# The end of a decoder step: written ahead of the branch for left-over blocks and once more behind it, with one tile summed on TensorE

## The chip, the cores and the metric

The kernel runs on one core of a Trainium2 chip. The metric is device microseconds of one execution, the median of several runs. A profiled execution of the same program gives the trace that is read here; its times count from the start of its span.

## The reference, cut to what matters

The whole step is one decoder layer: a prompt of 512 rows and 8 sample rows of 1024 columns go through attention, a convolution group and a mixture of experts. Only its last lines are touched by the change:

```python
def rmsnorm(x, g):
    x32 = x.astype(jnp.float32)
    y = x32 * lax.rsqrt(jnp.mean(x32 * x32, axis=-1, keepdims=True) + EPS)
    return (y * g.astype(jnp.float32)).astype(x.dtype)
...
    x = x + mods[2] * mix
    h = rmsnorm(x, norm2_g) * (1.0 + mods[4]) + mods[3]
    return x + mods[5] * hier_moe(h, ...)      # top 2 of 8 experts in the best of 4 groups
...
    y_prompt = rmsnorm(xp, final_g)
    y_sample = rmsnorm(xs, final_g)
```

Every row gets the products of two experts. The sum of the residual row and its two expert rows is scaled by the inverse root of its mean square and by `final_g`.

## The kernel before, in words

Everything is in one core's program; a framework orders the instructions of each engine by its own model of time and puts in the semaphores. Where the order of one engine matters the code pins it with `tc.issue_after`.

**The expert loop.** Rows are grouped by expert into blocks of 64. There are 32 experts and four static second blocks, 36 blocks in all (`OV0`), and up to 16 more (`MAXX`) for rows that did not fit. `run` (L1611) goes through the 36: `weights` (L1530) reads 3 MB for each expert on SyncE's queue into pages, a rotating pool of 21 buffers (`page`, L195); `turned` and `up` make the two hidden products on TensorE, `hidden` (L1575) a Silu on ScalarE and a product on VectorE, `flip` and `down` the last product. `down` scatters the block's result from `ot` into the DRAM tensor `yrow`, with an indirect DMA on Pool's queue (L1600). `yrow` has four rows of 512 columns for every token: two experts times two halves. The residual is in the DRAM tensor `xrow`.

**The left-over blocks.** After the loop `gf` (`final_g`) and the four residual tiles `xt` are asked for on SyncE. All engines read a count (`nxi`, L1798) and branch on it (L1799). If it is over 0 the 16 left-over blocks run with weights gathered by indirect DMAs. With the inputs given it is 0 and the blocks are skipped. What a skipped block would have counted up on the semaphores is made up for at the end of the branch, at the same line.

**The end.** Behind the branch come L1805 to L1863. The 512 prompt rows are four tiles of 128 rows and 1024 columns. SyncE reads, for each, two halves of `yt` (L1813, one for each expert, 512 KB), and after tile 1's the eight sample rows in four small DMAs (`ysq`, L1816). `total(i)` (L1820) adds the two halves to the residual on VectorE (L1822, L1826), ScalarE squares and sums the result (L1827), VectorE adds EPS (L1832 or L1830) and Pool takes the power -1/2 (L1833). `final(i)` (L1836) scales on VectorE (L1845) and SyncE writes the tile out (L1846). Tile 3 goes in two halves of 512 columns. `sample` (L1848) adds the sample rows on Pool in three operations of 256 columns; `quarter_rstd` (L537) squares them on ScalarE (L540), adds partitions with a small product (L542) and ends in `rsq` (L333), with a power on Pool (L336). VectorE scales them (L1860) and ScalarE's queue writes them in four small DMAs (L1863). The order is "t0 t1 f0 t2 f1 s t3 q f2 f3"; only VectorE's sums, and the finals, the sample and its root against the sum before them, are pinned. L1883 is the closing of the program: drains of all engines and a handshake.

In the middle of the kernel, `tile_start(2)` (L1367) asks for output weights and `mrow`'s rows, and Pool clears the half page `B2b` (L1386, `mB` in the trace), which the expert loop later uses for gathered rows.

Of the kernel before, what the change touches and what calls it, by code (L numbers as in the profile page):

```python
# [9 lines left out]
F32 = mybir.dt.float32  # L10
# [4 lines left out]
ALU = mybir.AluOpType  # L15
# [14 lines left out]
GF_ = ()  # L30
ORD, ISS = "t0 t1 f0 t2 f1 s t3 q f2 f3", "fsq"
GT, TH, TF = (), (1, 1, 1, 2), (1, 1, 1, 2)
# [148 lines left out]
def body(tc, I, O, dbg=lambda *a: None):  # L181
# [13 lines left out]
    def page(name, w=2048):  # L195
        t = pg.tile([128, PW], F32, tag="E", name=name)
        return t[:, :w]
# [1169 lines left out]
    def tile_start(i):  # L1367
# [15 lines left out]
        if i == WOI:  # L1383
            load_wo(0, 2)
            SP.dma_start(A2b, mrow[2:3, :].to_broadcast([128, 1024]))
            G.memset(B2b, 0.0)  # L1386
            for q in range(4):
                SP.dma_start(b2q[32 * q:32 * q + 8].rearrange("p (c j) -> p c j", c=8),
                             mrow[1:2, :].rearrange("o (c r j) -> o c r j", r=4, j=32)[:, :, q].to_broadcast([8, 8, 32]))
            ready.add("A")  # L1390
# [184 lines left out]
    def hidden(b):  # L1575
        pgu = pgus.pop(b)
        hd = hds[b] = small("hd")
        S.activation(hd[64:128], pgu[0:64], AF.Silu)  # L1578
        return V.tensor_tensor(hd[64:128], pgu[64:128], hd[64:128], op=ALU.mult)  # L1579
# [54 lines left out]
    pgus, hds, hTs_, scat = {}, {}, {}, []  # L1634
# [153 lines left out]
    run(todo, asked)  # L1788
    gfq = cp.tile([128, 256], F32, name="gfq", tag="c1")
    with tc.issue_after(mark["S"].ins):  # L1790
        S.dma_start(gfq, I["GFQ"])
# [3 lines left out]
    for i in range(4):  # L1795
        SP.dma_start(half(xt[i // 2], i % 2), xrow[128 * i:128 * i + 128])
    spare = [[page(f"sg{j}"), page(f"su{j}"), page(f"sd{j}")] for j in range(3)]
# [5 lines left out]


    ry = yrow.rearrange("(t a) f -> t (a f)", a=4)  # L1805
    ssf = cp.tile([128, 8], F32, name="ssf")
    rsf = cp.tile([128, 8], F32, name="rsf")
    ysq = mid("ysq").rearrange("p (a f) -> p a f", a=2)
    V.memset(ysq, 0.0)
    yt = [page(f"yt{i}") for i in range(4)]  # L1810
    for i in range(4):
        for j in range(2):
            SP.dma_start(half(yt[i], j), ry[128 * i:128 * i + 128, 1024 * j:1024 * j + 1024])  # L1813
        if i == 1:
            for q in range(4):
                SP.dma_start(ysq[32 * q:32 * q + 8].rearrange("p a (c j) -> p (a c) j", c=8),  # L1816
                             ry[512:520].rearrange("b (x r j) -> b x r j", r=4, j=32)[:, :, q])
    fs = small("fs")

    def total(i):  # L1820
        t, t1, x = half(yt[i], 0), half(yt[i], 1), half(xt[i // 2], i % 2)
        (G if i in GT else V).tensor_tensor(x, x, t, op=ALU.add)  # L1822
        n = 1024 // TH[i]
        for h in range(TH[i]):
            c = slice(n * h, n * h + n)
            op = V.tensor_tensor(t[:, c], x[:, c], t1[:, c], op=ALU.add)  # L1826
            S.activation(t1[:, c], t[:, c], AF.Square, scale=1.0 / 32, accum_out=ssf[:, 2 * i + h:2 * i + h + 1])  # L1827
        r = rsf[:, i:i + 1]
        if TH[i] == 2:
            V.scalar_tensor_tensor(r, ssf[:, 2 * i:2 * i + 1], EPS, ssf[:, 2 * i + 1:2 * i + 2], op0=ALU.add, op1=ALU.add)  # L1830
        else:
            V.tensor_scalar(r, ssf[:, 2 * i:2 * i + 1], EPS, None, op0=ALU.add)  # L1832
        G.tensor_tensor(r, r, mh[:, 0:1], op=ALU.pow)  # L1833
        return op

    def final(i):  # L1836
        n = 1024 // TF[i]
        for h in range(TF[i]):
            c = slice(n * h, n * h + n)
            t = half(yt[i], 0)[:, c]  # L1840
            if i in GF_:
                S.activation(t, t, AF.Copy, scale=rsf[:, i:i + 1])
                G.tensor_tensor(t, t, gfb[:, c], op=ALU.mult)
            else:
                V.scalar_tensor_tensor(t, t, rsf[:, i:i + 1], gfb[:, c], op0=ALU.mult, op1=ALU.mult)  # L1845
            SP.dma_start(O[0][0, 128 * i:128 * i + 128, c], t)  # L1846

    def sample():  # L1848
        G.tensor_tensor(fs, ysq[:, 0], ysq[:, 1], op=ALU.add)  # L1849
        G.tensor_tensor(fs, fs, m5s, op=ALU.mult)  # L1850
        G.tensor_tensor(fs, fs, x1s, op=ALU.add)  # L1851

    op = None
    for nm in ORD.split():
        with tc.issue_after(op.ins) if op is not None and nm[0] in ISS else ExitStack():
            r = (sample() if nm == "s" else quarter_rstd(rsf[:, 4:5], fs, 1.0 / D, EPS) if nm == "q" else
                 total(int(nm[1])) if nm[0] == "t" else final(int(nm[1])))
        if nm[0] == "t":
            op = r
    V.scalar_tensor_tensor(fs, fs, rsf[:, 4:5], gfq, op0=ALU.mult, op1=ALU.mult)  # L1860
    oq = O[1].rearrange("b t (c r j) -> (b t) c r j", r=4, j=32)
    for q in range(4):
        S.dma_start(oq[:, :, q], fs[32 * q:32 * q + 8].rearrange("p (c j) -> p c j", c=8))  # L1863
# [23 lines left out]
```

## Time and profile before

| | us |
|---|---|
| median of 3 runs | 795.29 (792.6 to 795.43) |
| the profiled execution | 790.3 |
| its span | 788.4 |
| PE busy | 688.5 (87%) |
| DVE busy | 452.7 (57%) |
| ACT busy | 205.8 (26%) |
| POOL busy | 203.0 (26%) |

PE is TensorE, DVE VectorE, ACT ScalarE, POOL Pool (GpSimd) and SP SyncE; a name with q is the engine's queue of DMA issues, semaphores and branches. PEclk is the share of TensorE's full clock that was granted. The span is a little shorter than the execution's time, since it runs from the first to the last instruction of the program. The shares of busy time are averages over stages with different limits, so the rows below are from the last 40 us, where the change plays, and a few from other stages for the price of single operations.

### The profile page before, as it was taken

The numbers are of one execution on the slowest core, as the hardware profiler recorded it, in microseconds if no ns is written. First come the engines' busy times: TensorE is split into PE (matmuls) and PEld (weight loads), VectorE is DVE, ScalarE is ACT, GpSimd is POOL, SyncE is SP. The second block draws the span as 40 slices with busy tenths as digits, with TensorE's granted clock in tenths as the row PEclk, the third lists the DMA queues.
The fourth block names the chain that finished last, engine by engine and source line by source line (L and its number), as shares of the span: only waits on it lengthen the run. The fifth ranks groups of instructions, "written<-read, shape, count | busy, mean of one in ns | idle before, by whom it ended". The sixth has DMA issues, their size and how long they took to land. (4 is left out here: it accounts for less than half of the span.)

```text
span 788.4 us, 12678 instructions
## 1 busy us (share of the span) xinstructions
PE 688.5 (87%) x4908; PEld 416.2 (53%) x4908; DVE 452.7 (57%) x995; ACT 205.8 (26%) x475; POOL 203.0 (26%) x183
## 2 busy tenths in 40 slices
PE   5999898998999988999789998389999999999800
PEld 3555887877786445544445445245555555554400
DVE  3445629999984758732777744664444434343335
ACT  1254721111122557543235324020000000000011
POOL 5144205034230101135610202112222222221114
PEclk9999999999998999999979999599999999999965
DMA  9985325645899104500003857789998999999853
GB/s 344 419 347 201 135 81 216 243 160 219 280 382 402 62 2 149 240 0 1 1 16 137 317 194 277 276 307 398 418 380 322 416 418 420 416 419 419 351 195 147
DMA packets 42477, 199.54 MB, mean 253 GB/s; under 512 B 11005, under 2 KB 14477, under 8 KB 22821
## 3 DMA queue, kind: packets, MB, share of 16 engines
q1 hardware_dynamic: 29485, 155.78, 50.8%
q0 software_dynamic: 10336, 40.95, 13.4%
q10 hardware_dynamic: 2592, 1.95, 0.8%
q8 instruction: 41, 0.67, 0.3%
q14 instruction: 23, 0.19, 0.1%
HBM read 187.33 MB, written 22.15 MB: 266 GB/s over the span
## 5 line engine op out<-in xcount | busy, mean ns | idle before, releaser
L591 DVE SCALAR_TENSOR_TENSOR y<-u,c,y 128x511 f32<-128x511 f32 (+23 forms) x120 | 102.0, 882 | 2.1
L1578 ACT ACTIVATE hd<-pgu 64x256 f32<-64x256 f32 x36 | 13.5, 376 | 234.8 <-PE pgu L1573 234.8
L1600 POOL DMA_INDIRECT yrow<-ot,six x36 | 39.2, 1088 | 99.3 <-DVE ot L1599 88.2
L1573 PE MATMUL pgu<-eu,mB 128*64 128x256 f32 x256 | 61.7, 384 | 1.6 <-DMA eu<-in_WU 1.5
L1573 PE MATMUL pgu<-eg,mB 128*64 128x256 f32 x256 | 62.1, 384 | 0.0
L1595 PE MATMUL pd<-ed,hTe 128*64 128x512 f32 x240 | 57.3, 598 | 0.8 <-issue 0.8
L1573 PE MATMUL pgu<-eu,mA 128*64 128x256 f32 x224 | 54.0, 384 | 1.9 <-DMA eu<-in_WU 1.9
L1573 PE MATMUL pgu<-eg,mA 128*64 128x256 f32 x224 | 54.2, 384 | 0.0
L1579 DVE TENSOR_TENSOR hd<-pgu,hd 64x256 f32<-64x256 f32 x36 | 15.4, 428 | 52.4 <-ACT hd L1578 52.3
L1599 DVE SCALAR_TENSOR_TENSOR ot<-pd,wtb,mt 128x512 f32<-128x512 f32 x36 | 27.0, 751 | 31.2 <-PE pd L1595 31.2
L1573 PEld LDWEIGHTS pgu<-eg,mB 128*64 128x64 f32 x256 | 32.9, 136 | 19.7 <-issue 5.9
L225 DVE COPY hTe<-hTp 128x128 f32<-128x128 f32 x36 | 10.5, 291 | 50.2 <-PE hTp L1586 48.9
L1573 PEld LDWEIGHTS pgu<-eg,mA 128*64 128x64 f32 x224 | 28.8, 136 | 17.1 <-issue 5.2
L1423 ACT ACTIVATE P<-pSp,ast 128x128 f32<-128x128 f32 (+3 forms) x64 | 33.2, 535 | 17.3 <-DVE ast L1418 17.0
L370 PE MATMUL pr<-cTs,wc 128*64 128x256 f32 x256 | 36.1, 390 | 0.0
L1418 DVE TENSOR_REDUCE ast<-pSp 128x1 f32<-128x384 f32 (+3 forms) x44 | 27.3, 633 | 14.4 <-PE pSp L1413 14.3
L1573 PEld LDWEIGHTS pgu<-eu,mB 128*64 128x64 f32 x256 | 33.0, 136 | 3.7 <-DMA eu<-in_WU 2.5
L1292 PE MATMUL woA<-wo,qT 128*128 128x512 f32 x64 | 34.3, 652 | 0.2 <-DVE x1a L1295 0.2
L1573 PEld LDWEIGHTS pgu<-eu,mA 128*64 128x64 f32 x224 | 28.9, 136 | 3.5 <-DMA eu<-in_WU 2.5
L1112 PE MATMUL woC<-wo,y 128*128 128x512 f32 x64 | 30.6, 608 | 0.1
L361 PE MATMUL cT<-CI,cR 128*128 128x128 f32 x128 | 20.9, 300 | 10.4 <-DVE cR L386 10.3
L542 PE MATMUL qs<-st,CI 128*128 128x1 f32 x6 | 1.5, 311 | 31.1 <-ACT jks L540 31.1
(582 smaller groups left out, 1694.3 us busy)
## 6 DMA issues: line engine op xcount, KB each, us to landing
eg<-in_WG SPq DMA_DIRECT2D x26, 1024.0 KB
eu<-in_WU SPq DMA_DIRECT2D x26, 1024.0 KB
ed<-in_WD SPq DMA_DIRECT2D x26, 1024.0 KB
wada<-in_WA SPq DMA_DIRECT2D x16, 1024.0 KB
wada<-in_WA POOLq DMA_DIRECT2D x8, 1024.0 KB
WG<-in_WG SPq DMA_DIRECT2D x6, 1024.0 KB
WU<-in_WU SPq DMA_DIRECT2D x6, 1024.0 KB
WD<-in_WD SPq DMA_DIRECT2D x6, 1024.0 KB
```

What stands on the lines that cost most here:

```text
L361: PE.transpose(p[:, j, :], R[b:b + n, c, k, 2 * s8:2 * s8 + 2, :], ident[b:b + n, b:b + n])
L370: mark["PE"] = PE.matmul(self.pr[r][64 * c:64 * c + 64], wc1[:, c, 8 * r + 4 * h + s, :], self.T[h][:, c, s], start=(h == 0 and s == 0), s ...
L591: V.scalar_tensor_tensor(yb[:, s_:CVS], ub[:, :CVS - s_], w(k), yb[:, s_:CVS], op0=ALU.mult, op1=ALU.add)
L1112: PE.matmul(p, zc[:, g, 128 * i:128 * i + 128], wo[2 * n + 1][:, g], start=(g == 0), stop=(g == 3))
L1292: PE.matmul(pA, oTp[:, g, 128 * i:128 * i + 128], wo[2 * n][:, g], start=(g == 0), stop=(g == 3))
L1418: V.tensor_reduce(st[k][:, 0, h0:h0 + nh], pS[k][:, :nh * L].rearrange("p (h l) -> p h l", h=nh), axis=AX.X, op=ALU.max, negate=True)
L1423: S.activation(P[k][:, g, :L], pS[k][:, o:o + L], AF.Exp, bias=st[k][:, 0, g:g + 1], accum_out=st[k][:, 1, g:g + 1])
L1573: chain[0] = PE.matmul(pgus[b][64 * h:64 * h + 64, :], xT[:, c, 64 * s_:64 * s_ + 64], w[:, c, :], start=(c == 0), stop=(c == 7))
L1579: return V.tensor_tensor(hd[64:128], pgu[64:128], hd[64:128], op=ALU.mult)
L1595: chain[0] = PE.matmul(pd[64 * h:64 * h + 64, :], hT_[:, c, :], wd[:, c, 512 * h:512 * h + 512], start=(c == 0), stop=(c == 1))
L1599: V.scalar_tensor_tensor(ot, pd, wtb[:, b:b + 1], mt, op0=ALU.mult, op1=ALU.mult)
L1600: st = G.indirect_dma_start(out=yrow[:, :], out_offset=bass.IndirectOffsetOnAxis(ap=six[:, b:b + 1], axis=0), in_=ot, in_offset=None, boun ...
```

## The change

The end, from the reads of `yt` to the writes, becomes a function `ending`, called twice: right after the 36 blocks, ahead of the count and the branch, and again inside the branch after the left-over blocks, which then writes all outputs anew. So that the first call reads no rows that were never written, SyncE fills `yrow` with zeros from `B2b` in `tile_start(2)`.

Inside `ending`: tile 0 is summed on TensorE as three products with the identity for each half of 512 columns (residual, first expert, second expert) in PSUM; tiles 1 to 3 on VectorE in halves. Each tile of `yt` is read in one DMA of 1 MB. Pool has no work: the sample's three sums are on VectorE, and the power is replaced by `inv_root`, a square root on ScalarE and, on VectorE, a reciprocal with one step of Newton's method. All of VectorE's operations are pinned in the order of the program by `dv`, all of ScalarE's activations by `ac`. One square root of a constant is put behind the loop's last Silu.

```diff
@@ head of the file
-ORD, ISS = "t0 t1 f0 t2 f1 s t3 q f2 f3", "fsq"
+TP = (0,)
@@ tile_start
             G.memset(B2b, 0.0)
+            SP.dma_start(yrow.rearrange("(p a b) f -> p a (b f)", p=104, b=2), B2b[:104].unsqueeze(1).to_broadcast([104, 10, 1024]))
             for q in range(4):
@@ hidden
-        S.activation(hd[64:128], pgu[0:64], AF.Silu)
+        silu[0] = S.activation(hd[64:128], pgu[0:64], AF.Silu)
@@ behind run(todo, asked)
-    with tc.issue_after(mark["S"].ins):
+    with tc.issue_after(silu[0].ins):
         S.dma_start(gfq, I["GFQ"])
...
+    with tc.issue_after(mark["V"].ins):
+        V.memset(ysq, 0.0)
+    with tc.issue_after(silu[0].ins):
+        S.activation(rsf[:, 5:6], one, AF.Sqrt)
+
+    def ending():
+        for i in range(4):
+            SP.dma_start(half(xt[i // 2], i % 2), xrow[128 * i:128 * i + 128])
+        for i in range(4):
+            SP.dma_start(yt[i], ry[128 * i:128 * i + 128])
+            if i == 1:
+                for q in range(4):
+                    SP.dma_start(ysq[32 * q:32 * q + 8].rearrange("p a (c j) -> p (a c) j", c=8),
+                                 ry[512:520].rearrange("b (x r j) -> b x r j", r=4, j=32)[:, :, q])
+        row, arow = [None], [None]
+        def ac(*a, **k):
+            with tc.issue_after(arow[0].ins) if arow[0] is not None else ExitStack():
+                arow[0] = S.activation(*a, **k)
+        def dv(f, *a, **k):
+            with tc.issue_after(row[0].ins) if row[0] is not None else ExitStack():
+                row[0] = f(*a, **k)
+        def inv_root(s_, r, t):
+            ac(t[:, 0:1], s_, AF.Sqrt)
+            dv(V.reciprocal, t[:, 1:2], t[:, 0:1])
+            dv(V.scalar_tensor_tensor, t[:, 0:1], s_, t[:, 1:2], t[:, 1:2], op0=ALU.mult, op1=ALU.mult)
+            dv(V.tensor_scalar, t[:, 0:1], t[:, 0:1], -0.5, 1.5, op0=ALU.mult, op1=ALU.add)
+            dv(V.tensor_tensor, r, t[:, 0:1], t[:, 1:2], op=ALU.mult)
+        py = {i: [acc("py") for _ in range(2)] for i in TP}
+        with in_turn():
+            for i in TP:
+                for h, c in enumerate(cols):
+                    chain[0] = PE.matmul(py[i][h], ident, half(xt[i // 2], i % 2)[:, c], start=True, stop=False)
+        def total(i, hs=(0, 1)):
+            t0, t1, x = half(yt[i], 0), half(yt[i], 1), half(xt[i // 2], i % 2)
+            for h in hs:
+                c = cols[h]
+                if i in TP:
+                    with in_turn():
+                        PE.matmul(py[i][h], ident, t0[:, c], start=False, stop=False)
+                        chain[0] = PE.matmul(py[i][h], ident, t1[:, c], start=False, stop=True)
+                    z = py[i][h]
+                else:
+                    dv(V.tensor_tensor, x[:, c], x[:, c], t0[:, c], op=ALU.add)
+                    dv(V.tensor_tensor, x[:, c], x[:, c], t1[:, c], op=ALU.add)
+                    z = x[:, c]
+                ac(jy[:, c], z, AF.Square, scale=1.0 / 32, accum_out=ssf[:, 2 * i + h:2 * i + h + 1])
+        def root(i):
+            s_ = ssf[:, 2 * i:2 * i + 1]
+            dv(V.scalar_tensor_tensor, s_, s_, EPS, ssf[:, 2 * i + 1:2 * i + 2], op0=ALU.add, op1=ALU.add)
+            inv_root(s_, rsf[:, i:i + 1], rtt[:, i])
+        def final(i):
+            for h, c in enumerate(cols):
+                z = py[i][h] if i in TP else half(xt[i // 2], i % 2)[:, c]
+                o = half(yt[i], 0)[:, c]
+                dv(V.scalar_tensor_tensor, o, z, rsf[:, i:i + 1], gfb[:, c], op0=ALU.mult, op1=ALU.mult)
+                if i > 1:
+                    SP.dma_start(O[0][0, 128 * i:128 * i + 128, c], o)
+            if i < 2:
+                SP.dma_start(O[0][0, 128 * i:128 * i + 128], half(yt[i], 0))
+        total(0)
+        total(1)
+        root(0)
+        final(0)
+        total(2)
+        root(1)
+        final(1)
+        dv(V.tensor_tensor, fs, ysq[:, 0], ysq[:, 1], op=ALU.add)
+        dv(V.tensor_tensor, fs, fs, m5s, op=ALU.mult)
+        dv(V.tensor_tensor, fs, fs, x1s, op=ALU.add)
+        ac(jks, fs, AF.Square, accum_out=rtt[:, 5, 0:1])
+        total(3)
+        p = tps("qs", (128, 1))
+        PE.matmul(p, sel, rtt[:, 5, 0:1], start=True, stop=True)
+        root(2)
+        dv(V.tensor_scalar, rtt[:, 5, 1:2], p, 1.0 / D, EPS, op0=ALU.mult, op1=ALU.add)
+        inv_root(rtt[:, 5, 1:2], rsf[:, 4:5], rtt[:, 4])
+        final(2)
+        dv(V.scalar_tensor_tensor, fs, fs, rsf[:, 4:5], gfq, op0=ALU.mult, op1=ALU.mult)
+        for q in range(4):
+            S.dma_start(oq[:, :, q], fs[32 * q:32 * q + 8].rearrange("p (c j) -> p c j", c=8))
+        root(3)
+        final(3)
+
+    ending()
+
+    spare = [[page(f"sg{j}"), page(f"su{j}"), page(f"sd{j}")] for j in range(2)]
     nxv = nc.values_load(nxi[0:1, 0:1])
     with tc.If(nxv > 0):
         chain[0] = None
         gather(OV0 // 2)
         run([(b, lambda b=b: left(b - OV0)) for b in range(OV0, NBLK)], asked)
+        ending()
...
```

What is left out: the removed code of the end (it stands above, L1805 to L1863), and the new tiles that `ending` uses (`ssf`, `rsf`, `rtt`, `ysq`, `fs`, `yt` and others), which are taken ahead of it.

## Rows read from the trace of the kernel before

**Rows 1.** Windows: length, busy time of PE, PEld, DVE, ACT, POOL, granted clock, DMA share, GB/s.
```profile
397.00:404.00 7.00, 6.59 (x11) 2.98 (x11) 3.69 (x9) 1.91 (x6) 0.55 (x1) 0.53 0.01 2
527.00:750.00 223.00, 218.73 (x1572) 113.85 (x1570) 90.74 (x178) 12.78 (x34) 54.76 (x50) 1.00 0.98 395
...
757.00:782.00 25.00, 0.58 (x2) 0.50 (x2) 17.18 (x21) 5.18 (x12) 9.86 (x8) 0.50 0.65 237
```

**Rows 2.** The chain that ended last: start, length, what.
```profile
751.72 5.21 DMA yrow<-ot,six
...
757.00 0.32 SPq L1813
```

**Rows 3.** The branch's line L1799: queue, operation, count, duration in ns, when.
```profile
L1799 SPq COMPARE_BRANCH  x1: 50/50/50, 737.2 to 737.2; - x1
...
L1799 PEldq COMPARE_BRANCH  x1: 3443/3443/3443, 749.3 to 749.3; - x1
...
L1799 POOLq INC_SWDGE_SEM  x1: 1996/1996/1996, 755.0 to 755.0; - x1
```

**Rows 4.** DMA queues in 752.6 to 754.2: packets, MB, share.
```profile
q0 software_dynamic: 80, 0.03, 7.4%
```

**Rows 5.** DMA in 754.2 to 757.9 (the one packet is code).
```profile
DMA packets 1, 0.01 MB, mean 2 GB/s; under 512 B 0, under 2 KB 0, under 8 KB 0
```

**Rows 6.** Timeline of VectorE at the end: start, length, line, operation, wait before it.
```profile
762.47 1.23 DVE L1826 TENSOR_TENSOR yt<-xt,yt 128x1024 f32<-128x1024 f32 x1 [0.22 <-DMA ysq<-yrow]
...
765.81 1.23 DVE L1826 TENSOR_TENSOR yt<-xt,yt 128x1024 f32<-128x1024 f32 x1 [0.46 <-DMA ysq<-yrow]
...
776.65 1.29 DVE L1826 TENSOR_TENSOR yt<-xt,yt 128x512 f32<-128x512 f32 x2
...
779.64 0.48 DVE L1860 SCALAR_TENSOR_TENSOR fs<-fs,rsf,gfq 128x256 f32<-128x256 f32 x1 [0.37 <-POOL rsf L336]
780.16 1.41 DVE L1845 SCALAR_TENSOR_TENSOR yt<-yt,rsf,gf 128x512 f32<-128x512 f32 x2
```

**Rows 7.** Timeline of ScalarE at the end.
```profile
763.78 1.06 ACT L1827 ACTIVATE yt<-yt 128x1024 f32<-128x1024 f32 x1 [17.43 <-DVE yt L1826]
...
774.99 0.42 ACT L540 ACTIVATE jks<-fs 128x256 f32<-128x256 f32 x1 [6.77 <-POOL fs L1851]
...
777.37 0.63 ACT L1827 ACTIVATE yt<-yt 128x512 f32<-128x512 f32 x1 [0.84 <-DVE yt L1826]
...
780.16 3.42 ACTq L1863 DMA_DIRECT2D out<-fs  x4
```

**Rows 8.** Timeline of Pool, its last operation.
```profile
779.58 0.54 POOL L1833 TENSOR_TENSOR rsf<-rsf,mh 128x1 f32<-128x1 f32 x1
```

**Rows 9.** The closing L1883: count, duration in ns (least, median, most), first and last start.
```profile
L1883 POOLq DRAIN  x3: 51/109/8253, 779.3 to 788.1; - x3
L1883 SPq DRAIN  x3: 7/7/13, 785.5 to 787.8; - x3
```

**Rows 10.** The count's line L1798 on SyncE.
```profile
L1798 SPq TENSOR_LOAD <-nxi x1: 277/277/277, 736.9 to 736.9; - x1
```

**Rows 11.** Timeline of VectorE at 519, a small operation.
```profile
519.52 0.19 DVE L1748 RECIPROCAL rt<-rt 128x5 f32<-128x5 f32 x1
```

**Rows 12.** Timeline of ScalarE at 517.
```profile
517.50 0.19 ACT L1745 ACTIVATE rt<-rt 128x5 f32<-128x5 f32 x1
517.70 1.28 ACT L1578 ACT_TABLE_LOAD   x1
```

**Rows 13.** The page's costliest groups: products of 128x512 at L1292.
```profile
L1292 PE MATMUL woA<-wo,qT 128*128 128x512 f32 x64 | 34.3, 652 | 0.2 <-DVE x1a L1295 0.2
```

**Rows 14.** Timeline of TensorE behind an idle stretch.
```profile
398.65 5.25 PE L1292 MATMUL woA<-wo,qT 128*128 128x512 f32 x6
```

**Rows 15.** Timeline of Pool at 340.
```profile
340.37 0.95 POOL L1386 MEMSET mB<- 128x1024 f32 x1
```

**Rows 16.** DMA in 341 to 356.
```profile
DMA packets 0, 0.00 MB, mean 0 GB/s; under 512 B 0, under 2 KB 0, under 8 KB 0
```

More of the change, by code (lines that the diff above doesn't have):

```diff
@@ L29 @@
 KTE = "VSSSSVVSSSSSSSVSSSSVVSSS"
-GF_ = ()
-ORD, ISS = "t0 t1 f0 t2 f1 s t3 q f2 f3", "fsq"
-GT, TH, TF = (), (1, 1, 1, 2), (1, 1, 1, 2)
+TP = (0,)
 PLAN = ",c0,spread gn im sel,,,c1,k0 n cp,,,mc,,sn n3 n1 n0 n2,k1 rw,,,nq,,,,,,,,,,,,,cs,"
@@ L1632, in run @@
         down(*before)
-    pgus, hds, hTs_, scat = {}, {}, {}, []
+    pgus, hds, hTs_, scat, silu = {}, {}, {}, [], [None]
     asked = {0, 1, OV0 // 2, NBLK // 2}
@@ L1794, in body @@
     xt = [page("xt0"), page("xt1")]
-    for i in range(4):
-        SP.dma_start(half(xt[i // 2], i % 2), xrow[128 * i:128 * i + 128])
-    spare = [[page(f"sg{j}"), page(f"su{j}"), page(f"sd{j}")] for j in range(3)]
+    ry = yrow.rearrange("(t a) f -> t (a f)", a=4)
+    ssf = cp.tile([128, 8], F32, name="ssf")
+    rsf = cp.tile([128, 8], F32, name="rsf")
+    rtt = cp.tile([128, 8, 2], F32, name="rtt")
+    yp, jy = page("ysq"), page("jy")
+    ysq, fs, jks = yp[:, 0:512].rearrange("p (a f) -> p a f", a=2), yp[:, 512:768], yp[:, 768:1024]
@@ new lines, in body @@
+    oq = O[1].rearrange("b t (c r j) -> (b t) c r j", r=4, j=32)
+    yt = [page(f"yt{i}") for i in range(4)]
+    cols = [slice(512 * h, 512 * h + 512) for h in range(2)]
+    with tc.issue_after(mark["V"].ins):
[79 more added lines that the diff above has]
+        final(3)
@@ L1802, in body @@
         run([(b, lambda b=b: left(b - OV0)) for b in range(OV0, NBLK)], asked)
[L1805 to L1861, printed above, removed]
@@ L1862, in body @@
-    for q in range(4):
-        S.dma_start(oq[:, :, q], fs[32 * q:32 * q + 8].rearrange("p (c j) -> p c j", c=8))
+        ending()
     es.close()
```

## The prediction

> **What bounds the kernel now.** I first read the windows of the end [rows 1]. Up to 750 us the expert loop streams weights (DMA share 0.98, 395 GB/s) and TensorE runs at the granted clock 1.00. From 757 to 782 TensorE is busy for 0.58 us, and VectorE for 17.18 of 25 us, at a granted clock of 0.50, which is 1.2 GHz. So the change plays in a stretch of some 37 us of which VectorE sets most.
>
> Next the chain of waits [rows 2]. It begins with a scatter into `yrow` that seems to take 5.21 us, and only then are `yt` rows asked for. The branch's own rows [rows 3] show something else in this time: Pool spends 2.00 us from 755.0 on an increment of its DMA semaphores. That stands in for the scatters of the blocks not run, and ends at 757.0, when the reads start. The DMA queues tell where the scatter's bytes really were: 80 packets of queue q0 between 752.6 and 754.2 [rows 4], and no data at all from 754.2 to 757.9 [rows 5]. So some 2.6 us belong to the branch and not to the scatter.
>
> Then VectorE up to 782 [rows 6]: two sums of 1024 columns for a tile (1.23 us each), a scaling, and so on without long gaps until 781.57. Of the waits, tile 0 has both its halves when L1826 starts at 762.47, tile 1 at 765.81, that is 5.5 and 8.8 us after the first read is issued. ScalarE [rows 7] squares 512 columns in 0.63 us and at last issues four `out<-fs` DMAs, 3.42 us for all. Pool's last power [rows 8] ends at 780.12, yet its DRAIN [rows 9] ends at 779.3 + 8.25 = 787.6, while SyncE's has begun by 785.5 with all writes landed. The last 0.8 us to 788.4 are the closing handshake. So Pool's drain ends last, 2 us after everything else.
>
> **The change part by part.** *Earlier reads.* The reads no longer stand behind the branch. Issued at 754.4 instead of 757.0 they put tile 0 at 759.9 and tile 1 at 763.2, by the distances above. The bounds: 0 if the 5.21 us were the scatter itself, and 3.2 if the bytes count from 753.8.
>
> *The closing.* Nothing is left on Pool after its branch, so a drain of 7.45 us (780.12 to 787.6) would end near 765. Between 0 and 2.0 us are saved; I take all, because the drain follows Pool's last instruction and none of the DMAs. The branch now comes after the ending: SyncE reads the count in 0.28 us [rows 10] and branches in 0.05 [rows 3]. TensorE, whose branch cost 3.44 us, is done early. From VectorE's last operation I count 0.4 for the last write's issue, 1.95 for its landing (before, from 783.58, where the last `out<-fs` issue ends, to 785.5 [rows 7, 9]), 0.35 for count and branch, 0.5 for the semaphores of the DMAs not issued (an estimate; Pool's like step took 2.0) and 0.8: 4.0 us, bounds 3.5 and 5.5, against 6.8 (781.57 to 788.4) now.
>
> The Trainium skill (Runtime: NRT & Kernel Launch, Instruction fetch mechanics) says that a taken branch whose target lies outside the loaded window waits for a fetch; TensorE's 3.44 us against SyncE's 0.05 fits, and were it VectorE's or SyncE's turn at the end, up to 3.4 us would come on top.
>
> *Less adding on VectorE, more small steps.* Tile 0's two sums (2.5 us) go to TensorE. The other three tiles are summed in halves, four operations; two such take 1.29 back to back now [rows 6], and with the wait of a dependent one I take 0.7 for each but 0.61 for a free one: 2.7 us a tile. A scaling stays 1.4. The three sample sums come over from Pool, where ScalarE waited 6.77 us for them [rows 7]; on VectorE a 256-column operation is 0.48 at most [rows 6], so 1.4. What is new is the root. Before, Pool made a power beside VectorE's other work. Now every tile, and the sample, takes one small VectorE step, a square root on ScalarE and four more VectorE steps, and the order is fixed: VectorE's next operation stands behind them. A small step lasts 0.19 at most [rows 11], 0.2 with the wait for the one before it, and a small activation 0.19 [rows 12]. So a root costs 0.2 + 0.25 + 0.8 = 1.25, and as the root of a tile also queues behind the last square of the sum before it (0.75, of which 0.2 hides the first step), 1.8 from the end of a sum. Five roots are 6 to 8 us of which nothing lies beside other work.
>
> *Tile 0 on TensorE.* A 128x512 product shows as two instructions: 64 for the 32 products of L1292 [rows 13]. After an idle stretch, at the clock of 0.53 between 397 and 404 [rows 1], six of them take 5.25 us [rows 14], 0.86 each. TensorE will be idle from about 752.4 (the two `xt` products run directly after the loop) until 759.9, as long as it idles now before the stretch from 757 on with its 0.50 [rows 1]. So four products take 6.9 us, 3.4 at 2.4 GHz; I take 6.9. ScalarE's order is fixed too, and tile 1's squares wait behind tile 0's.
>
> *ScalarE's table.* One small square root after the last Silu loads the table, 1.28 us [rows 12], where ScalarE is idle for 17.43 us before its first square [rows 7]: hidden. *The four `out<-fs` issues* stand in ScalarE's program ahead of tile 3's square root and are ready first, when the sample is scaled. If they go first, the last root waits 3.4 us more; bounds 0 and 3.4. I take 3.4.
>
> *Zeros into `yrow`.* SyncE writes 4.26 MB (2080 rows of 2 KB) after Pool's memset of `mB`, at 340.37 to 341.3 [rows 15]. At 395 GB/s that is 11 us, and from 341 to 356 no DMA moves a byte [rows 16], so nothing that stands behind it on SyncE's queue is due by then; the first scatter comes in the expert loop, long after. Cost nothing; without the idle queues up to 11. The other new loop work (a 0.48 us memset, the table, two products after the last block) lies on engines with slack.
>
> **The sum**, on the profile's clock. Tile 0 is summed at 766.9. Three squares in a row (0.63 each) end at 768.8, square root and four steps at 769.9. Scaling 771.3; sum of tile 2 774.0; root 775.8; scaling 777.2; sample sums 778.6; sum of tile 3 781.3; root 783.1; sample's root 784.3; scaling 785.7; sample scaled 786.1; four issues 789.5; last root 790.6; last scaling 792.0; end 796.0, against 788.4. That is 7.6 us; I round to 7.2, as tile 2 and 3's first step may hide behind the squares. The profiled execution took 790.3 us, 1.9 more than its span, and the median of the runs is 795.29, 5 above it; the difference is put on the median: 802.5 us. A run of this kernel can be told from no change by some 0.5%, so below 791.3 is faster and above 799.3 slower.
>
> **The rivals.** *The four issues do not stand ahead of the last square root.* Then the last root follows at once: 802.5 - 3.4 = 799.1. This ends within 0.5%. Its place is ScalarE's queue at about 786, and it decides as soon as the square root is ahead of the first issue. For it: in the trace of before ScalarE's order was not the program's either; it waited 6.77 us for the sample's square [rows 7], which the program has behind tile 2's. Against: the issues are both earlier in the program and ready earlier.
>
> *Early tiles.* If the reads run at the loop's rate at once, 2.65 us for 1 MB, tile 0 lands at 758.0 and tile 1 at 760.7, and with TensorE at 2.4 GHz the first root ends at 765.2, not 769.9: 797.8, and 794.4 with the rival before. For it: nothing else is on the queues. Against: tile 0's halves took 5.5 us in just this setting, and the clock.
>
> *The change does not free the reads.* If the 5.21 us were the scatter's own landing, they stay at 757.0: 805.1. Against it stand the packets [rows 4, 5].
>
> *Tables.* ScalarE now alternates squares and square roots, and if each change loaded a table, six loads of 1.28 us would fall on VectorE's chain: 7.7 us, 810. Against it: squares ran after the Silu table and no load is seen among them [rows 7, 12]. The Trainium skill (ScalarE: Activation LUTs, Table sets: the hidden batching unit) asks to batch activations by set, since each change of set loads one; it speaks against the change if squares were not in the square root's set, and its page does not list them there.
>
> **How the numbers follow.** Forecast 0.45, issues not ahead 0.25, early tiles 0.17, reads not freed 0.08, tables 0.05. The forecast's own range, with its bounds (the clock, the closing, small steps at 0.15 to 0.22), is 798.5 to 806. Slower: 0.42 of the forecast, 0.10 of the issues, 0.03 of the early tiles, 0.07 and 0.05 of the last two: 0.67. Faster: 0.05, the early tiles with the four issues behind and a closing of 3.5 and less. The rest is 0.28. The range leaves out the tables and the lower half of the early tiles: 794 to 806.5.
>
> **What would show it.** Right: the first `yt` issue near 754.4; no Pool work behind the branch and its DRAIN no longer last; VectorE waiting for ScalarE five times, about 0.5 to 1 us each; products of tile 0 at 0.86 us an instruction and granted clock 0.50; four `out<-fs` issues ahead of the last square root; the loop up to 750 unchanged. Wrong: VectorE's last scaling before 785, a table load behind the first, a SyncE queue held up at 341, or an end set by VectorE's or SyncE's branch.

## The result and the profile after

The change makes the kernel slower: 804.52 us median (801.47 to 807.29, 4 runs) against 795.36 (792.6 to 797.52, 4 runs), ratio 1.0114 [1.0074, 1.0153]. The forecast was 802.5 and slower.

| | before | after |
|---|---|---|
| the profiled execution | 790.3 | 803.69 |
| its span | 788.4 | 801.9 |
| the last scatter starts (S) | 751.72 | 758.93 |
| VectorE's last scaling ends, from S | +29.85 | +37.71 |
| the span ends, from S | +36.71 | +42.97 |

The two profiled executions lie 13.4 us apart, but 7.2 of that is there before the end begins. But for the added instructions, every engine goes through the same order up to the last scatter, and most of the 7.2 us is older than all of these: VectorE's first reduction of L1418 starts at 303.7 before and at 309.4 after, while the zeros are issued at 347.1. Windows with the same work in both, with the columns of [rows 1], first two of the kernel before, then two of the changed one:

```profile
244.00:310.00 66.00, 59.05 (x522) 33.45 (x519) 44.92 (x104) 34.43 (x81) 8.23 (x8) 1.00 0.27 105
530.00:751.72 221.72, 216.38 (x1552) 112.11 (x1548) 88.58 (x170) 12.78 (x34) 53.51 (x50) 1.00 0.97 393
```

```profile
246.00:316.00 70.00, 63.07 (x521) 35.55 (x519) 45.25 (x106) 34.73 (x83) 8.25 (x8) 0.94 0.25 96
537.00:758.93 221.93, 217.51 (x1553) 112.48 (x1550) 89.04 (x171) 14.25 (x36) 53.30 (x50) 1.00 0.97 392
```

The expert loop takes as long in both, at the same clock; 4 us are lost between 246 and 316, where the granted clock is 0.94 instead of 1.00. Why the clock differs there from run to run was not looked into. In the 13 profiles of this study, one of each kernel, S lies anywhere between 751.7 (the kernel before) and 762.3, without a visible order by what was edited: 760.8 with the zeros alone, 754.1 and 758.9 with the zeros and more. So all that follows counts from S, the start of the last scatter into `yrow`. By this measure the change costs 42.97 - 36.71 = 6.3 us. The ratio's interval is 5.9 to 12.2 us.

A window of the changed kernel at the same place behind S as 757 to 782 in [rows 1]:

```profile
764.00:789.00 25.00, 5.93 (x10) 2.58 (x10) 14.55 (x37) 6.58 (x22) 0.00 (x0) 0.64 0.54 199
```

In the same 25 us VectorE has 37 operations instead of 21, and is busy for 14.55 us instead of 17.18: it waits more, though Pool's 9.86 us of work are gone. The timeline of the changed kernel from the scatter to the first sums shows how the end begins:

```profile
758.93 0.98 POOL L1600 DMA_INDIRECT yrow<-ot,six  x1 [1.79 <-DVE ot L1599]
761.46 0.80 SPq L1815 DMA_DIRECT2D yt<-yrow  x2
...
766.78 2.07 PE L1852 MATMUL py<-yt,CI 128*128 128x512 f32 x2 [7.01 <-DMA yt<-yrow]
768.65 1.76 PE L1853 MATMUL py<-yt,CI 128*128 128x512 f32 x2
770.25 1.02 PE L1852 MATMUL py<-yt,CI 128*128 128x512 f32 x2
...
770.82 2.74 DVE L1829 TENSOR_TENSOR xt<-xt,yt 128x512 f32<-128x512 f32 x4 [12.17 <-DMA ysq<-yrow]
...
771.11 1.02 PE L1853 MATMUL py<-yt,CI 128*128 128x512 f32 x2
```

The first read is issued 2.53 us behind S, not 5.28 as in [rows 2]. TensorE starts on tile 0 at 766.78 and is done at 772.13; the first four instructions take 3.5 us, the last four 1.9. And VectorE idles for 12.17 us, until tile 1 has landed (at 770.25; the row names the first of the sample's reads, which landed at 770.65). Two windows in these products, with the columns of [rows 1]:

```profile
766.80:770.20 3.40, 3.40 (x4) 1.49 (x5) 0.00 (x0) 0.00 (x0) 0.00 (x0) 0.51 1.07 292
770.30:772.10 1.80, 1.80 (x5) 0.52 (x3) 1.25 (x2) 0.69 (x2) 0.00 (x0) 1.00 1.01 401
```

The granted clock is 0.51 (1.2 GHz) in the first, and from 770.3 on 1.00 (2.4 GHz), after TensorE had been busy without a gap since 766.78.

The same timeline, further on, with VectorE's waits for ScalarE:

```profile
774.50 0.16 DVE L1829 RECIPROCAL rtt<-rtt 128x1 f32<-128x1 f32 x1 [0.87 <-ACT rtt L1825]
...
775.39 1.41 DVE L1829 SCALAR_TENSOR_TENSOR yt<-py,rsf,gf 128x512 f32<-128x512 f32 x2
...
788.63 0.16 DVE L1829 RECIPROCAL rtt<-rtt 128x1 f32<-128x1 f32 x1 [0.27 <-ACT rtt L1825]
...
791.18 2.93 ACTq L1896 DMA_DIRECT2D out<-ysq  x4
794.15 0.20 ACT L1825 ACTIVATE rtt<-ssf 128x1 f32<-128x1 f32 x1 [5.56 <-DMA out<-ysq]
794.39 0.16 DVE L1829 RECIPROCAL rtt<-rtt 128x1 f32<-128x1 f32 x1 [3.17 <-ACT rtt L1825]
...
795.23 1.41 DVE L1829 SCALAR_TENSOR_TENSOR yt<-xt,rsf,gf 128x512 f32<-128x512 f32 x2
```

The wait of 0.87 comes three times (tiles 0 to 2), 0.27 for the sample, and 3.17 for tile 3, whose square root stands behind the four `out<-fs` issues (the page that holds `fs` is called `ysq` now). Last the branch L1904 and the closing L1928, to be read against [rows 3, 9]:

```profile
L1904 SPq EVENT_SEMAPHORE  x8: 17/17/17, 797.8 to 800.2; - x8
...
L1904 POOLq INC_SWDGE_SEM  x1: 1996/1996/1996, 762.1 to 762.1; - x1
L1904 PEldq COMPARE_BRANCH  x1: 3892/3892/3892, 785.1 to 785.1; - x1
...
L1928 POOLq DRAIN  x3: 51/103/7418, 764.2 to 801.6; - x3
L1928 SPq DRAIN  x3: 7/7/13, 801.0 to 801.3; - x3
```

Pool's drain of 7.42 us now ends at 771.6 and sets nothing; TensorE's long branch lies beside VectorE's work. SyncE goes through eight semaphore steps from 797.8 to 800.2 and drains at 801.0. Most of that is waiting: by SyncE's waits in 795 to 802 (total, times, longest) 2.2 us at these steps, and the last two writes move their 0.52 MB until 799.2.

```profile
SPq L1904 <- SPq L1904: 2.2, 4, 0.8
```

### The profile page after: what moved, and what is told of

Same layout as the page of the kernel before. It is cut to its first block, busy times and chain, and to the rows that moved or that the text cites. A ratio compares the mean times of both kernels' runs of the same rounds, so it can differ in the third digit from the quotient of the medians.

```text
span 801.9 us, 12737 instructions
## 1 busy us (share of the span) xinstructions
PE 702.1 (88%) x4920; PEld 422.0 (53%) x4920; DVE 454.6 (57%) x1024; ACT 208.8 (26%) x488; POOL 192.6 (24%) x175
## 3 DMA queue, kind: packets, MB, share of 16 engines
q0 software_dynamic: 10336, 40.95, 13.2%
q10 hardware_dynamic: 2592, 1.95, 0.8%
## 5 line engine op out<-in xcount | busy, mean ns | idle before, releaser
L1423 ACT ACTIVATE P<-pSp,ast 128x128 f32<-128x128 f32 (+3 forms) x64 | 33.2, 535 | 18.5 <-DVE ast L1418 18.2
L1418 DVE TENSOR_REDUCE ast<-pSp 128x1 f32<-128x384 f32 (+3 forms) x44 | 27.3, 633 | 15.7 <-PE pSp L1413 14.3
L1455 PE MATMUL oT<-P,kv 128*64 128x512 f32 x80 | 28.5, 614 | 0.0
```

The costliest lines, as they stand in the source:

```text
L1418: V.tensor_reduce(st[k][:, 0, h0:h0 + nh], pS[k][:, :nh * L].rearrange("p (h l) -> p h l", h=nh), axis=AX.X, op=ALU.max, negate=True)
L1423: S.activation(P[k][:, g, :L], pS[k][:, o:o + L], AF.Exp, bias=st[k][:, 0, g:g + 1], accum_out=st[k][:, 1, g:g + 1])
L1455: PE.matmul(oT[64 * k:64 * k + 64, :].rearrange("p (g t) -> p g t", g=4), kv12[:, br - 1, kt, 128 + 64 * k:192 + 64 * k], P[k][:, :, 128 * ...
```

## The experiments

The kernels of a group ran on one chip, with the kernel before beside them. The first group shared a median of before of 796.57 (33 runs), the second 795.23 (26), the third 794.80 (28).

**The issues behind the last root.**

```diff
-        for q in range(4):
-            S.dma_start(oq[:, :, q], ...)
         root(3)
         final(3)
+        with tc.issue_after(arow[0].ins):
+            for q in range(4):
+                S.dma_start(oq[:, :, q], ...)
```

> The change, but the four out<-fs issues stand on ScalarE's queue behind the last square root. Theory (the time is lost in VectorE's pinned chain of roots, and in the issues that stand ahead of the last one): VectorE's wait before the last reciprocal falls from 3.17 to about 0.3 us and its last scaling comes 2.9 us earlier; from the start of the last scatter to the end of the span 43.0 falls to about 40.5, so the time falls by 2 to 3 us against the change. Rival (the time is lost ahead of the end, in the loop or by the zeros): the wait falls too, but that stretch is not what makes the difference, and the time stays within 1 us of the change.

Measured: 799.79 (12 runs), ratio 1.0043 [1.0014, 1.0071]; VectorE ends at +35.61, the span at +41.08. ScalarE's timeline at the end:

```profile
788.41 0.20 ACT L1825 ACTIVATE rtt<-ssf 128x1 f32<-128x1 f32 x1 [2.65 <-DVE ssf L1829]
788.42 2.93 ACTq L1899 DMA_DIRECT2D out<-ysq  x4
```

The square root is first now, and VectorE's last wait is 0.27 instead of 3.17. So 2.9 us of the change's loss are these four issues. The end gained only 1.9, since in this run TensorE's eight instructions for tile 0 took 6.5 us at a granted clock of 0.56 and were done at +14.3, 1.1 later.

**The zeros alone**, put into the kernel before:

```diff
+            SP.dma_start(yrow.rearrange("(p a b) f -> p a (b f)", p=104, b=2), B2b[:104]...)
```

> The kernel before, with the zeros written into yrow and nothing else. Theory: no time, within 0.3% of the kernel before (795); 4.26 MB move between 340 and 360 us while no other DMA does, and the last scatter starts where it did, within the spread of the runs. Rival (the 7.2 us by which the last scatter starts later in the changed kernel's profile come from the zeros, or from the shift of the DMA semaphores that they cause): 3 to 7 us slower than the kernel before.

Measured: 793.69 (12 runs), ratio 0.9974 [0.9941, 1.0007]; the end 35.78 behind S. The issue, and the DMA queue in 341 to 366 (packets, MB, share):

```profile
347.68 0.97 SPq L1387 DMA_DIRECT2D yrow<-mB  x1
```

```profile
q1 hardware_dynamic: 783, 3.19, 51.3%
```

The write is slower than I reckoned: some 200 GB/s, and by 366 only 3.19 of the 4.26 MB are out. It costs nothing all the same: in the kernel before no data moves from 341 to 400, so no transfer is due while it runs. The end of this run is that of the kernel before, and 0.9 us shorter; so much can two profiles of one end differ.

**The new end once, behind the branch**, with the zeros kept:

```diff
-    ending()
     with tc.If(nxv > 0):
         ...
-        ending()
+    chain[0] = None
+    ending()
```

> The change's arithmetic at the old place: the ending once, behind the branch (zeros still written). Theory: the first read comes 5.3 us after the last scatter's start, not 2.5, the closing loses the count and the semaphore steps (about 1 us), so from the last scatter to the end 43.0 becomes 44.5 to 45, some 1.7 us slower than the change. Rival (what costs time is that the branch now stands behind the ending): 1 to 3 us faster than the change.

Measured: 803.85 (10 runs), ratio 1.0092 [1.0062, 1.0122]; the first read at +5.56, VectorE ends at +42.29, the span 45.53 behind S. Three lines of its timelines:

```profile
753.09 1.28 ACT L1825 ACT_TABLE_LOAD   x1 [0.24 <-ACTq L1902]
...
762.29 0.80 SPq L1815 DMA_DIRECT2D yt<-yrow  x2
...
774.83 1.28 ACT L1825 ACT_TABLE_LOAD   x1
```

VectorE's chain ends 4.6 us later than in the change. About 3 of them are the reads that wait for the branch. 1.3 are a table load that the change does not have at this place, and 0.5 the four issues, 3.43 us here instead of 2.93. Behind the branch ScalarE loads twice, although a table was warmed ahead of it: at 753.09, before its first square, where it is hidden, and again at the first square root.

**The old end ahead of the branch**, Pool's work and all:

```diff
+    def ending():
+        ...   # reads, total, final, sample and rsq of the kernel before
+    ending()
     with tc.If(nxv > 0):
         ...
+        ending()
```

> The old arithmetic at the new place: the old end, with Pool's powers and sums and with halves of yt, written ahead of the branch and once more behind it. Theory: the reads start 2.7 us earlier and VectorE's chain keeps its 20.5 us, but Pool's last power is now followed by the count, the branch, 2.0 us of increments and a drain of 7.4 us: from the last scatter to the end 36.7 - 2.7 + 5.2 = 39 us, 2 to 3 us slower than before and some 4 faster than the change. Rival (Pool's drain ends with the last landing and costs nothing): 2 us faster than before. Rival (upstream): as slow as the change.

Measured: 795.77 (12 runs), ratio 0.9994 [0.9962, 1.0027]; reads at +2.34, VectorE ends at +27.76, 2.1 earlier than before; the span 37.26 behind S. Its last power on Pool, then the branch and the closing:

```profile
779.82 0.55 POOL L1834 TENSOR_TENSOR rsf<-rsf,mh 128x1 f32<-128x1 f32 x1
```

```profile
L1865 POOLq INC_SWDGE_SEM  x1: 1996/1996/1996, 781.0 to 781.0; - x1
```

```profile
L1889 POOLq DRAIN  x3: 46/103/7418, 783.1 to 791.0; - x3
L1889 SPq DRAIN  x3: 7/7/13, 786.3 to 790.7; - x3
```

SyncE is ready at 786.3, but Pool goes power, increment, drain, one behind the other, to 790.5. What the earlier reads give, Pool's end takes back. The expected 39 was 1.7 too much: this kernel is not 2 to 3 us slower than the one before but level with it. The reads and the missing drain of Pool belong together all the same: to use the first one has to have Pool done early.

**No tile on TensorE.**

```diff
-TP = (0,)
+TP = ()
```

> The changed kernel, but tile 0 is summed on VectorE like the other three; no product in the ending. All times from the last scatter's start, S. Theory (the tile on TensorE gains nothing, since VectorE has nothing to do until tile 1 has landed, at +11.9 in the changed kernel): the 2.7 us of sums of tile 0 fit between its landing at +7.9 and +10.6, the squares and the root follow, and the first scaling is again at about +16.4 or a little earlier; end within 1 us of the changed kernel's 43.0 us behind S, time near 804. Rival (the tile on TensorE takes 2.5 to 2.7 us off VectorE's chain): the first scaling at about +19, end at 45.6, some 2.7 us slower than the changed kernel.

Measured: 800.18 (12 runs), ratio 1.0064 [1.0034, 1.0095]; the span 42.27 behind S, 0.7 less than in the change. VectorE's timeline, where S is 755.55:

```profile
763.35 2.75 DVE L1829 TENSOR_TENSOR xt<-xt,yt 128x512 f32<-128x512 f32 x4 [8.07 <-DMA yt<-yrow]
766.75 2.75 DVE L1829 TENSOR_TENSOR xt<-xt,yt 128x512 f32<-128x512 f32 x4 [0.65 <-DMA yt<-yrow]
...
771.27 1.41 DVE L1829 SCALAR_TENSOR_TENSOR yt<-xt,rsf,gf 128x512 f32<-128x512 f32 x2
```

Tile 0's sums fit into the time in which VectorE has nothing else, and there are 0.65 us to spare. The first scaling comes at +15.7 instead of +16.5: the tile on TensorE gained nothing.

**The roots on Pool.**

```diff
-            ac(t[:, 0:1], s_, AF.Sqrt)
-            dv(V.reciprocal, ...)          # and three steps more
+            G.tensor_tensor(r, s_, mh[:, 0:1], op=ALU.pow)
```

> The changed kernel with each root made as one power on Pool, as in the kernel before, instead of a square root on ScalarE and four steps on VectorE; no square root is left and so no table for it. Theory (a root on ScalarE and VectorE costs 1.8 us of the chain, a power on Pool some 0.8 of which VectorE is free to go on only if the order lets it; and the four issues no longer stand ahead of a square root): VectorE's last scaling ends at about +30 to +33 behind S instead of +37.7; but Pool's last power now ends late, and its fixed drain (7.42 us) with the semaphore step of the branch behind it sets the end: last power + 0.5 + 2.0 + 7.4 + 0.8, some 39 to 41 behind S, against 43.0. So 2 to 4 us faster than the changed kernel, still slower than before. Rival (the roots cost nothing): VectorE's last scaling at +37 and the end at 46 or later, 3 us slower than the changed kernel.

Measured: 800.63 (12 runs), ratio 1.0048 [1.0018, 1.0079]; VectorE ends at +29.60, the span at +39.58. The first root in the timeline, and the closing:

```profile
776.51 0.57 POOL L1831 TENSOR_TENSOR rsf<-ssf,mh 128x1 f32<-128x1 f32 x1 [13.20 <-DVE ssf L1827]
...
777.12 1.41 DVE L1827 SCALAR_TENSOR_TENSOR yt<-py,rsf,gf 128x512 f32<-128x512 f32 x2 [0.69 <-POOL rsf L1831]
```

```profile
L1922 POOLq DRAIN  x3: 46/103/7418, 793.7 to 801.6; - x3
```

A root now costs VectorE a small step and a wait of 0.69, and its chain is 8.1 us shorter than the change's. The span gains only 3.4 of them, because Pool's drain runs from 793.7 to 801.1. This is the run that shows where the loss lies: in the roots, the issues in front of the last one included (these alone are the 2.9 of the first run).

**The sample first, on a queue of its own.**

```diff
+            for q in range(4):
+                S.dma_start(ysq[32 * q:32 * q + 8]..., ry[512:520]...)
...
+        # sums, square, root, scaling of the sample ahead of total(0)
+            SP.dma_start(oq[:, :, q], ...)
```

> The changed kernel with the sample's part (reads, three sums, square, root, scaling, four out<-fs writes) taken out of the middle of the order: its rows are read first, by four DMAs on ScalarE's queue, its chain is made on VectorE before any tile has landed, and its four writes are issued by SyncE. Theory (1.3 us of sums, a root of 1.1, a scaling of 0.4 and the four issues of 2.9 stood on the chain that ends last): VectorE's last scaling ends at about +32 behind S instead of +37.7, the span ends 37.3 us behind S, some 6 us less than in the changed kernel and about level with the kernel before. Rival (only the issues count, the sample's small steps lie in waits anyway): last scaling at +35, as in the run with the issues last, 2 to 3 us faster than the changed kernel. Against both: the four more reads ahead of the tiles delay these, and the first tile's sum comes later by as much.

Measured: 806.22 (6 runs), ratio 1.0138 [1.0094, 1.0182]; VectorE ends at +44.23. A clear miss. VectorE's first operation, and the DMA queues in 767 to 771 (packets, MB, share):

```profile
776.16 0.43 DVE L1829 TENSOR_TENSOR ysq<-ysq 128x256 f32<-128x256 f32 x1 [16.98 <-DMA ysq<-yrow]
```

```profile
q1 hardware_dynamic: 209, 1.57, 97.3%
q10 hardware_dynamic: 99, 0.01, 2.2%
```

The sample's 65 KB are 512 packets of 128 bytes on ScalarE's queue q10, beside 512 packets of 8 KB for the tiles on SyncE's q1. While both have work, q10 gets through one packet for two of q1's, and so it creeps at the pace of 4.19 MB: the sample's first packet moves at 766.2, 4 us behind its first issue, some 225 of the 512 only after 774, and the last one 0.4 us after the tiles' last. VectorE starts 14 us behind the first issue. The Trainium skill (DMA: Bandwidth & Descriptors, Queues, rings and completion order) says that each DMA engine takes turns between the queues that have work, a packet of some 9 to 17 descriptors at a time. Turns fit these counts; how long one is they do not show, since the trace does not name the engine that moved a packet.

**The sample first, on one queue.** The same kernel, but SyncE issues the sample's reads ahead of the tiles'.

> The version with the sample first, but its four reads are issued by SyncE ahead of the tiles' reads, on the same queue, instead of by ScalarE beside them. Theory (in that run the sample's 512 packets of 128 bytes took turns with the tiles' packets of 8 KB, so 65 KB took as long as 4 MB, and that alone spoiled it): the sample has landed at about +7 behind S, the tiles come 2.7 us later than in the changed kernel for the four issues of 0.65, the sample's sums, root, scaling and issues (5.7 us) are off the chain: VectorE's last scaling ends at about +34.7, the span 40 behind S, 9 us less than with the reads beside the tiles' and 3 less than in the changed kernel. Rival (small packets are slow by themselves): the sample lands at +12 or later and the end is no better than the changed kernel's 43.

Measured: 799.19 (12 runs), ratio 1.0054 [1.0020, 1.0088]; VectorE ends at +34.97, the span 40.00 behind S. Here S is 757.04:

```profile
759.60 2.88 SPq L1817 DMA_DIRECT2D ysq<-yrow  x4
762.58 2.04 SPq L1819 DMA_DIRECT2D yt<-yrow  x4
```

```profile
764.17 0.43 DVE L1829 TENSOR_TENSOR ysq<-ysq 128x256 f32<-128x256 f32 x1 [7.41 <-DMA ysq<-yrow]
```

The sample is there 7.1 us behind S instead of 16.7. So the packets are not slow by themselves; it was the sharing. VectorE's chain ends 2.7 us earlier than in the change, as reckoned: the sample's part leaves it, and the later tiles cost half of that again.

**A version from the parts.** The first try had the sample's reads on the queue of their own too, and fell with that:

> A version put together from the parts: the ending as in the changed kernel, once ahead of the branch and a second time behind it, and nothing on Pool; the sample first (as in the run before), tile 1 on TensorE instead of tile 0, each root begun as soon as its squares are there and finished behind other work of VectorE, the scalings placed between, all out<-fs issues on SyncE. Theory (what was lost is the roots' and the sample's latency on one fixed order, and what the reads ahead of the branch and the missing drain of Pool gain is kept): VectorE's last scaling ends at about +27 behind S, the span 32 to 33 behind S against 43.0 of the change and 36.7 of the kernel before: 4 to 5 us faster than before, ratio 0.994 to 0.995. Rival (the reads set the pace, the last tile's rows land too late for that): last scaling not before +30, no faster than before.

Measured: 801.01 (9 runs), ratio 1.0077 [1.0043, 1.0112]; VectorE's first sum at +16.6, its end at +37.19. The second goes back to the change's reads:

```diff
-TP = (0,)
+TP = (2,)
...
+        total(0); total(1, first half); begin(0); total(1, second half); sample's sums
+        finish(0); final(0); begin(1); finish(1); final(1)
+        total(3, first half); sample's square root; total(3, second half); sample's root, scaling, issues on SP
+        begin(3); squares of tile 2; finish(3); final(3, first half); begin(2); final(3, second half)
+        finish(2); final(2)
```

Here `begin` is the root's first step and the square root, `finish` the four steps behind it.

> A second version put together from the parts, after the run with the sample first had shown that its reads come late on a queue of their own: the reads in the order of the changed kernel again (tiles 0 and 1, sample, tiles 2 and 3), tile 2 on TensorE instead of tile 0, the sample's sums behind tile 1's, each root begun behind its squares and finished behind other work, out<-fs issued by SyncE, no Pool. Same arithmetic as the change. By the rows of the earlier runs: VectorE starts at +7.8 behind S, waits 0.65 for tile 1, then has 2.7 us for each of three tiles, 1.4 and 0.5 for the sample, 1.4 for each of four scalings, 1.0 for each of five roots and some 1.0 of waits: last scaling ends at +29.2. Theory (with no Pool at the end only VectorE's chain and a closing of 5.3 count): span 34.5 behind S, some 8 us less than in the changed kernel, 2 us less than before (ratio 0.997, within what can be told). Rival (tile 2's sum on TensorE at the lower clock is late for the last root): up to 2 us more, level with before.

Measured: 792.31 (12 runs), ratio 0.9963 [0.9931, 0.9994]; VectorE ends at +28.98, the span 34.12 behind S. VectorE's timeline, with S at 759.33:

```profile
774.33 0.43 DVE L1829 TENSOR_TENSOR ysq<-ysq,x1s 128x256 f32<-128x256 f32 x1
774.67 0.15 DVE L1829 RECIPROCAL rtt<-rtt 128x1 f32<-128x1 f32 x1
...
786.90 1.41 DVE L1829 SCALAR_TENSOR_TENSOR yt<-py,rsf,gf 128x512 f32<-128x512 f32 x2
```

Tile 0's reciprocal follows the sample's sum without a wait, since its square root was made beside tile 1's sums. The arithmetic, the place ahead of the branch and the idle Pool are those of the change, and the end is 8.9 us shorter. New are the order, tile 2 instead of tile 0 on TensorE, and SyncE as the issuer of the sample's writes; how much the order gives alone was not measured.

**And a shorter root:**

```diff
-            dv(V.reciprocal, t[:, 1:2], t[:, 0:1])
-            ...
+            dv(V.reciprocal, r, t[:, 0:1])
```

> The version of e9_order with a shorter root: square root on ScalarE and one reciprocal on VectorE, without the three steps that refine it (so the result is as exact as these two are). Theory (a step of 0.2 us on VectorE's chain costs 0.2 us): five roots with three steps less are 3.0 us: last scaling ends at +26.2 behind S, span 31.5 behind S, 5 us less than before (ratio 0.9935). Rival (the steps lie in VectorE's waits for ScalarE, TensorE or the reads): 1 us less than e9_order at most.

Measured: 789.78 (12 runs), ratio 0.9953 [0.9917, 0.9988]; VectorE ends at +26.11, the span 31.84 behind S, 4.9 less than before. This is the version that beats both kernels. It leaves out the step of Newton's method, so its roots are as exact as ScalarE's square root is.

The ends of the single profiles against the medians of many runs, both as differences to the kernel before:

| | end behind S, us | median, us |
|---|---|---|
| change (4 runs) | +6.3 | +9.2 |
| issues last | +4.4 | +3.2 |
| zeros alone | -0.9 | -2.9 |
| new end behind the branch | +8.8 | +7.3 |
| old end ahead | +0.6 | -0.8 |
| no TensorE | +5.6 | +5.0 |
| roots on Pool | +2.9 | +5.4 |
| sample first, own queue | +12.6 | +11.0 |
| sample first, one queue | +3.3 | +4.4 |
| first version | +5.3 | +5.8 |
| second version | -2.6 | -2.5 |
| with a short root | -4.9 | -5.0 |

They agree within 3 us, and the mean of the twelve differences between the columns is 0.1 us, so on the whole what was added ahead of S made nothing there slower, to about 1 us. The change's own four runs are the furthest off: 2.9 of its 9.2 us are not in its end and stay unexplained. By its end the change costs 6 us.

## Why the prediction was right, point by point

The direction, the mechanism and nearly the size were right: more small steps on one fixed order of VectorE's, with the earlier reads and the missing drain too small to pay for them. The end was to cost 7.6 us on the profile's clock and cost 6.3: VectorE was done 2.6 earlier than forecast, and the closing took 1.3 longer. That the median came out so close, 804.52 against 802.5, is in part luck, for 2.9 us of it are not in the end. The steps, each from the S of its own profile:

| step | predicted | measured |
|---|---|---|
| first read | +2.7 | +2.5 |
| tile 0 landed (first product) | +8.2 | +7.9 |
| tile 0 summed on TensorE | +15.2 | +13.2 |
| first root done | +18.2 | +16.4 |
| sum of tile 3 | +29.6 | +27.6 |
| sample scaled | +34.4 | +32.2 |
| four issues done | +37.8 | +35.2 |
| last scaling | +40.3 | +37.7 |
| end | +44.3 | +43.0 |

- *Reads ahead of the branch* (-2.6): right. They start 2.75 earlier, and the run with the new end behind the branch puts 3.0 us on it. Of the 5.21 us that the chain of waits puts down to the scatter [rows 2] about half were indeed the branch's, 2.00 of them Pool's increment.
- *TensorE's products at 1.2 GHz* (6.9 us): 5.35, mis-sized by 1.6, the largest error; another 0.3 is the earlier landing. The granted clock rose after the first four instructions, so the other four took 1.9 us. It is a matter of the run: with the issues last, the eight took 6.5. What I did not ask is what the tile on TensorE is worth: the forecast set VectorE free of 2.5 us where it waited for reads anyway.
- *The roots* (1.8 each from the end of a sum): right. From the end of tile 2's sums at 779.45 to the scaling at 781.23 are 1.8 us. By the run with the roots on Pool they and the issues in front of the last one are 8.1 us, which is the whole loss and more. With the old end at the same place VectorE is done at +27.76, another 1.8 us earlier than with the roots on Pool; the sample's sums, which came over from Pool, are 1.3 of these.
- *Four issues ahead of the last square root* (3.4): right in place, 2.93 in size. The rival that they would not stand there was wrong; the run that put them behind took them off.
- *The closing* (4.0, bounds 3.5 to 5.5): 5.26, mis-sized by 1.3. From the end of the last write's issue (797.0) to SyncE's drain I had 2.8 us, 1.95 of them for the landing and 0.5 for the semaphores of the skipped DMAs; it took 4.0. The eight steps span 2.4, but 2.2 of that is waiting, and the last write has landed only at 799.6, 2.6 behind its issue. So half of the error is the landing, and half what follows it up to the drain, 1.4 us where I had 0.85. This error and the one on TensorE offset each other in part.
- *Pool's drain off the end*: right, 7.42 us that end at 771.6.
- *Zeros for nothing*: right, though the write took far longer than the 11 us I gave it.
- *No table for each change from square to square root*: right. One load of 1.28 us at 753.55, none at the six changes behind it. The Trainium skill (ScalarE: Activation LUTs, Table sets: the hidden batching unit) gives the rule that a change of set costs a load; here square and square root did not change it.
- *TensorE's slow branch*: the prediction read it by the Trainium skill's rule on a taken branch out of the loaded window (Runtime: NRT & Kernel Launch, Instruction fetch mechanics) and left open whether VectorE's or SyncE's would be as slow at the end. It stayed with TensorE, 3.89 us beside VectorE's work, SyncE's took 0.05, as before, and VectorE's 0.07.

## What to carry to other kernels

When work is moved off a slow engine onto a tight one, count the latency of the new round trip at every place where a fixed order stands still for it: in the change's order five roots with 0.2 us steps, and the issues ahead of the last, cost VectorE 8.1 us more than powers on Pool. Begun early and finished behind other work the roots no longer wait, or 0.27 us, for the square root; their steps still count, and three steps less in each took 2.9 us off. An engine that idles for a transfer gained nothing here from being relieved in that time. And to compare two ends, count from the last common event and not from the start of the program.

## What the hardware showed that I had not expected

- Pool's drain at the end of the program takes 7.42 us behind whatever Pool did last: 764.15 to 771.57 in the change, from 783.1 with the old end, from 793.7 with the roots on Pool, 7418 ns each time; in the kernel before it shows 8.25 [rows 9], of which the first 0.8 lie beside the last power [rows 8]. Ahead of it, the semaphores of skipped indirect DMAs take 2.00 us. So in these kernels Pool's last operation should be some 10 us ahead of the program's end.
- Four transfers of 128-byte pieces, 65 KB in all, took 14 us on a queue of their own beside 4.19 MB on another, and 4.6 us from first issue to use when they went first on one queue.
- A table of ScalarE's that was warmed ahead of a branch did not serve behind it: in the run with the new end behind the branch two loads of 1.28 us follow, one ahead of the first square and one at the first square root. Which tables these were the trace does not show.
